# Wider opening matmuls, relu kept in PSUM, more idle matmuls, an output-weight split on VectorE and a changed work order in a fused attention-and-FFN block

## The chip, the cores and the metric

One core of a Trainium2 chip runs the whole kernel. The metric is the device time of one execution in microseconds (us), median of several runs.

## The reference

One encoder layer for 512 tokens of width 1024, in float32. The parts that the kernel's stages follow:

```python
mod = silu(c) @ w_ada + b_ada             # shift, scale, gate for both halves
h = rms_norm(x, norm1_g) * (1 + scale1) + shift1
proj = h @ w_in                           # qa ka va (8 heads of 64), qb kb vb (4 heads of 2x64),
                                          # indexer qi ki wi, gates (2 x 1024)
idx_score = sum_h wi_h * relu(qi_h . ki)  # per query and key; top 256 keys are kept for branch A
y_a = softmax(norm(qa).norm(ka)/8 - alibi, on the kept keys) @ va
y_b = rms_norm((softmax_1 - lam*softmax_2) @ vb)
merged = sigmoid(g_a) * (y_a @ w_up_a) + sigmoid(g_b) * (y_b @ w_up_b)
x = x + gate1 * (merged @ w_o)
h2 = rms_norm(x, norm2_g) * (1 + scale2) + shift2
out = x + gate2 * ((silu(h2 @ w_ff1) * (h2 @ w_ff3)) @ w_ff2)
```

## The kernel before

Every large product is made of three fp32r matmuls: each operand is split into a high half (a cast on ScalarE, `cp`) and a low half (the difference, on VectorE by `sb` or on GpSimd by `psub`), and `Bank.three` adds high x high, high x low and low x high in PSUM. Weights come from HBM in units of 128x1024 (`load`, tiles `raw`), and `split` makes tiles `whi` and `wlo` of them; `ON_DVE` lists the kinds of unit whose low half is made on VectorE, the others go to GpSimd.

The program is written as a list of operations with their inputs, outputs and a cost in ns. `Order.plan` simulates the engines with these costs, takes on each engine the ready operation with the lowest priority number, and so fixes the order of every engine's instructions. `moved(d)` shifts the priority of what is inside. The order on the chip is then fixed: an engine that waits for one instruction runs none of those behind it. PSUM has three pools: `mm` (4 banks), `sb` (2) and `tb` (2).

Stages, by the time of the profile:

1. Opening (0 to 58 us). x is normalised (`scale_x`; `XS` lists the row blocks that ScalarE scales, VectorE takes the others), and for each of 8 column blocks `cb` the conditioning columns are made (`ada_col`: two reductions over 512 KB each on VectorE), x is transposed and scaled (`make_h`), and TensorE adds the block's part of q and k of B heads 0 and 1 (`quad_mm`: 128x256 each, tiles `qb`, `kb`) and of the indexer (`stat_mm`, tile `idx`). Six `idle` matmuls in float32 run before the first real one.
2. Indexer scores and attention (58 to 310 us). `scores` multiplies q and k of the indexer, ScalarE writes the relu into an SBUF tile `relu`, VectorE weights and adds it; `select` finds the top 256 keys in 16 rounds on VectorE. The heads are `head_b` and `head_a`. `quad` makes the other q, k, v projections in matmuls of 256 columns, `quad_out` normalises and transposes them. `PROG` is the list that sets the order in which all this is created; between the heads stand gate projections (`g0` to `g15`).
3. Gates and up-projections (to 382 us), `gate` and `up`, with `ada_late` (`l2`, `l99`): it makes the gate row of the first half (`ada_row`) and then the eight conditioning columns of the second half (`ada_col(1, ...)`).
4. Output projection (382 to 439 us), tiles `wo`; `split_o` splits its weights, the low halves on GpSimd (`psub`).
5. FFN (439 to 795 us), tiles `ff`.

The lines that set the order in stages 2 and 3:

```python
PROG = """scores s8 g0 qb1 vb0 B1 vb1 B0 g3 qa0 g13 g12 kb1 ka0 s9 s8 s9 B2 va0 s99 s8 qa1 g10 B3 g8 ka1 A2 A0 A3 va1
A1 l2 A4 A6 l2 g2 g9 g5 A5 l2 A7 u0 g1 l2 u1 g11 g14 g7 g15 u2 u3 l2 l2 g4 g6 l2 u4 u5 u6 u7 l99"""
```

Of the kernel before, what the change touches and what calls it, by code (L numbers as in the profile page):

```python
# [20 lines left out]
NB = 4  # L21
# [13 lines left out]
QUADS = ["qb0", "kb0", "vb0", "qb1", "kb1", "vb1", "qa0", "ka0", "va0", "qa1", "ka1", "va1"]  # L35
# [3 lines left out]
PROG = """scores s8 g0 qb1 vb0 B1 vb1 B0 g3 qa0 g13 g12 kb1 ka0 s9 s8 s9 B2 va0 s99 s8 qa1 g10 B3 g8 ka1 A2 A0 A3 va1  # L39
A1 l2 A4 A6 l2 g2 g9 g5 A5 l2 A7 u0 g1 l2 u1 g11 g14 g7 g15 u2 u3 l2 l2 g4 g6 l2 u4 u5 u6 u7 l99"""  # L40
# [3 lines left out]
def _units():  # L44
    u = [("p", k) for k in range(8)]
    for w in PROG:
        if w in QUADS:
            u += [(w, 0), (w, 1)]
        elif w[0] == "g":
            u.append(("g", int(w[1:])))  # L50
        elif w[0] == "u":
            u.append(("up", int(w[1:])))
# [25 lines left out]
def _pack(inp):  # L78
# [8 lines left out]
    for i, u in enumerate(UNITS):  # L87
        if u[0] == "p":
            w = w_in[128 * u[1]:128 * u[1] + 128]
            w = np.concatenate([w[:, 3072:3396], w[:, 1536:1792], w[:, 2048:2304]], axis=1)  # L90
        elif u[0] in QUADS:
# [132 lines left out]
class Order:  # L224
# [56 lines left out]
    def plan(self, slots):  # L281
# [19 lines left out]
        while heap:  # L301
# [10 lines left out]
            for e in engs:  # L312
# [65 lines left out]
def _body(ctx: ExitStack, tc: tile.TileContext, a, out):  # L378
# [47 lines left out]
    def act(o, i, n, f=AF.Copy, bias=None, scale=1.0, accum=None, also=()):  # L426
        def fn():
# [4 lines left out]
            else:  # L432
# [3 lines left out]
                if accum is not None:  # L436
# [5 lines left out]
                  after=exps if f == AF.Sigmoid else (), table=table)  # L442
# [51 lines left out]
    def cp(o, i, n):  # L494
        act(o.r(), i, n)
# [156 lines left out]
    def make_h(cb):  # L652
# [3 lines left out]
        for p in range(pieces):  # L656
# [5 lines left out]
            cp(h, f[:, c].k(p), n)  # L662
            sb(l, f[:, c].k(p), h, n)

# [40 lines left out]
    def quad_out(name, banks):  # L705
        kind, br, n = name[0], name[1], int(name[2])
        if kind == "v":
            tl = []
            if br == "a":
                tl = [new("t", "va").rearrange("p (h x) -> p h x", h=4) for _ in range(NB)]  # L710
                src = [banks[t // 2][:, (t % 2) * 256:(t % 2) * 256 + 256].rearrange("p (h x) -> p h x", h=4) for t in range(NB)]
                for q in range(2):
                    for t in (2 * q, 2 * q + 1):
                        cp(tl[t][:, :, 0:64], src[t], 256)
                    for t in (2 * q, 2 * q + 1):
                        sb(tl[t][:, :, 64:128], src[t], tl[t][:, :, 0:64], 256)
            else:
                for q in range(2):
                    h, l = new("t", "vbh"), new("t", "vbl")
                    cp(h, banks[q], 512)  # L720
                    sb(l, banks[q], h, 512)
                    tl.append((h, l))
# [10 lines left out]
        for q in range(2):  # L733
# [3 lines left out]
            qn.append(s)  # L737
        res = []
        for pr in range(2):
            b = Bank("qkT", "tb")  # L740
            for t in range(NB):
                c = (t % 2) * 256 + pr * P
                b.tr(b[:, t * P:(t + 1) * P], qn[t // 2][:, c:c + P], ident)
# [21 lines left out]
    def gate_out(j, b):  # L765
        gates[j] = new("t", "gate")
        act(gates[j], b, 512)

# [20 lines left out]
    for cb in range(8):  # L789
        ada_col(0, cb)  # L790
        if cb == 7:
# [4 lines left out]
            act(csc, vec[:, V_CC:V_CC + 8], 8, AF.Silu)  # L796
# [3 lines left out]
        with G.moved(-H_MOVE if cb else 0):  # L800
            make_h(cb)
        if cb == 0:
            idle = Bank("idle")
            for _ in range(6):
                G.op("PE", 700, lambda: nc.tensor.matmul(g(idle[:, 0:256]), g(cs[:, 0:P]), g(cs[:, 0:256]), start=True, stop=True),
                     (cs,), (idle,))
            bi = [Bank("idx", x) for x in ("sb", "sb", "tb")]
            bq, bk = [Bank("qb0"), Bank("qb0")], [Bank("kb0"), Bank("kb0")]
# [11 lines left out]
    quad_out("qb0", bq)  # L820
    quad_out("kb0", bk)
# [27 lines left out]
    def scores(i):  # L849
        n = P * (i + 1)  # L850
        for h in range(4):
# [6 lines left out]
            r = new("s", "relu")  # L858
# [59 lines left out]
    def head_b(h):  # L918
        n, pr = h // 2, h % 2
        q, k, v = store[f"qb{n}"][pr], store[f"kb{n}"][pr], store[f"vb{n}"]  # L920
# [328 lines left out]
```

## Time and profile before

| what | value |
|---|---|
| runs | 801.61, 799.69 and 801.50 us, median 801.5 |
| profiled execution | 800.93 us, of which the span from first to last instruction is 799.1 us |
| TensorE busy | 781.9 us of the span, 4261 matmuls |
| VectorE, ScalarE, GpSimd busy | 456.2, 350.1 and 200.3 us |
| mean granted TensorE clock | 0.996 of full |

Busy time is a union of instructions. Matmuls overlap in the pipeline and their ends are modelled, so the distance from one matmul's start to the next one's is the better price of a matmul; an idle time that the profile shows for TensorE is a little shorter than the real one. PE is the matmul itself, PEld the weight load that overlaps it, DVE is VectorE, ACT ScalarE, POOL GpSimd.

### The profile page before, as it was taken

To read this page: it belongs to the slowest core of one execution; us is meant where nothing else is said; L and a number is where in the kernel's file an instruction comes from. 1 tells how busy PE (TensorE), PEld (TensorE's weight loads), DVE (VectorE), ACT (ScalarE), POOL (GpSimd) and SP (SyncE) were. 2 spreads that over 40 slices of the span, in tenths; PEclk is the share of its full clock that TensorE was granted. 3 is DMA by queue.
4 is the path that set the end of the run, shared out by engine and by line. 5 is a ranking of instruction groups with operands and counts; after the bars stand their busy time and mean duration, and the time that the engine had idled before them with its cause. 6 is when DMAs were issued, how large, how long until landed. Compare 5 with 4: busy or idle time off the path is not lost.

```text
span 799.1 us, 11091 instructions
## 1 busy us (share of the span) xinstructions
PE 781.9 (98%) x4261; PEld 673.9 (84%) x4261; DVE 456.2 (57%) x898; ACT 350.1 (44%) x649; POOL 200.3 (25%) x129
## 2 busy tenths in 40 slices
PE   7998999999999999999899999999999999999998
PEld 4997988999999888888688988888888888888886
DVE  5969999855468986277776524444433333212243
ACT  5566486357468777532436422332333322211310
POOL 1036554688464223453920000000000000000000
PEclk8999999999999999999999999999999999999999
DMA  9941222221233312457562223344432232232311
GB/s 348 398 136 53 81 69 65 80 80 65 83 107 117 106 55 87 149 185 279 168 237 80 80 106 112 129 154 153 138 105 85 101 106 84 100 106 85 126 40 66
DMA packets 29147, 97.97 MB, mean 123 GB/s; under 512 B 3235, under 2 KB 4771, under 8 KB 29094
## 3 DMA queue, kind: packets, MB, share of 16 engines
q1 hardware_dynamic: 28518, 96.35, 35.2%
q10 hardware_dynamic: 576, 0.92, 0.3%
q8 instruction: 33, 0.54, 0.3%
q14 instruction: 20, 0.16, 0.1%
HBM read 95.16 MB, written 2.10 MB: 122 GB/s over the span
## 4 chain that ended last, share of the span: by engine, by line
PE 85%; DVE 7%; issue 3%; DMA 2%; ACT 2%; POOL 1%; SPq 0%; POOLq 0%; ACTq 0%; DVEq 0%
PE ff L516 44%; PE gate L516 11%; PE up L516 5%; PE wo L516 3%; PE kb L516 3%; PE qa L516 3%; PE ka L516 2%; PE S L516 2%; PE PT L529 2%; PE qb L516 2%; PE idx L516 2%; PE PVa L516 1%; PE va L516 1%; PE vb L516 1%; DMA raw<-in_wun 1%
## 5 line engine op out<-in xcount | busy, mean ns | idle before, releaser
L429 ACT CAST whi<-raw 128x1024 fp32r<-128x1024 f32 x109 | 114.6, 1052 | 292.3 <-PE ff L516 148.2
L501 POOL TENSOR_TENSOR wlo<-raw,whi 128x1024 fp32r<-128x1024 f32 x46 | 114.9, 2499 | 157.9 <-ACT whi L429 133.3
L453 DVE TENSOR_TENSOR wlo<-raw,whi 128x1024 fp32r<-128x1024 f32 x63 | 77.1, 1225 | 117.4 <-ACT whi L429 114.6
L516 PE MATMUL ff<-h2l,whi 128*128 128x512 f32 (+1 forms) x384 | 142.5, 371 | 0.0
L516 PE MATMUL ff<-h2h,wlo 128*128 128x512 f32 (+1 forms) x384 | 142.4, 371 | 0.0
L516 PE MATMUL ff<-h2h,whi 128*128 128x512 f32 (+1 forms) x384 | 142.3, 372 | 0.0
L516 PE MATMUL ff<-whi,f 128*128 128x512 f32 (+1 forms) x310 | 95.1, 385 | 0.0
L516 PEld LDWEIGHTS ff<-h2l,whi 128*128 128x128 f32 x384 | 72.3, 188 | 12.5
L516 PEld LDWEIGHTS ff<-h2h,wlo 128*128 128x128 f32 x384 | 72.2, 188 | 12.5
L516 PEld LDWEIGHTS ff<-h2h,whi 128*128 128x128 f32 x384 | 72.2, 188 | 12.5
L516 PEld LDWEIGHTS ff<-whi,f 128*128 128x128 f32 x310 | 58.0, 188 | 11.6
L516 PE MATMUL ff<-wlo,f 128*128 128x512 f32 (+1 forms) x155 | 59.5, 385 | 0.0
L459 DVE TENSOR_TENSOR silu<-ff,silu 128x512 f32<-128x512 f32 x22 | 15.2, 692 | 69.4 <-PE ff L516 69.4
L516 PE MATMUL gate<-hh,whi 128*128 128x512 f32 x128 | 51.4, 402 | 0.0
L516 PE MATMUL gate<-hh,wlo 128*128 128x512 f32 x128 | 51.1, 401 | 0.0
L516 PE MATMUL gate<-hl,whi 128*128 128x512 f32 x128 | 51.0, 399 | 0.0
L473 DVE CUSTOM_DVE_ANT_0 raw<-raw,cs 128x1024 f32<-128x1024 f32 x32 | 45.7, 1440 | 4.2 <-DMA raw<-in_adat 2.7
L438 ACT ACTIVATE sx<-sx,nm 128x128 f32<-128x128 f32 (+3 forms) x64 | 35.7, 560 | 9.7 <-DVE nm L473 9.4
L482 POOL TENSOR_TENSOR r<-v,mhalf 128x16 f32<-128x16 f32 (+2 forms) x14 | 27.9, 1993 | 43.9 <-DVE v L463 40.3
L516 PEld LDWEIGHTS ff<-wlo,f 128*128 128x128 f32 x155 | 29.1, 188 | 5.9
L467 DVE SCALAR_TENSOR_TENSOR acc<-raw,csc,acc 128x1024 f32<-128x1024 f32 x16 | 20.7, 1294 | 22.0 <-DMA raw<-in_adar 21.9
L516 PE MATMUL wo<-wo,mh 128*128 128x512 f32 x96 | 30.2, 393 | 1.3 <-ACT mh L429 1.3
(229 smaller groups left out, 1708.0 us busy)
## 6 DMA issues: line engine op xcount, KB each, us to landing
raw<-in_wun SPq DMA_DIRECT2D x118, 512.0 KB, 3.3
raw<-in_adat SPq DMA_DIRECT2D x32, 512.0 KB, 7.3
raw<-in_adar SPq DMA_DIRECT2D x16, 512.0 KB, 3.3
x<-in_x SPq DMA_DIRECT2D x4, 512.0 KB, 5.9
praw<-in_wun SPq DMA_DIRECT2D x8, 256.0 KB, 7.4
xr<-in_x SPq DMA_DIRECT2D x4, 512.0 KB, 5.8
praw<-in_wun SPq DMA_DIRECT2D x8, 162.0 KB, 7.4
out_y<-out SPq DMA_DIRECT2D x4, 256.0 KB, 2.0
```

Of the source, the lines that this page charges most:

```text
L429: nc.scalar.copy(g(o), g(i))
L438: nc.scalar.activation(g(o), g(i), f, scale=g(scale), **kw)
L453: dve(n, False, lambda: nc.vector.tensor_sub(g(o), g(i), g(j)), (i, j), (o,), two=(i, j))
L459: dve(n, False, lambda: nc.vector.tensor_mul(g(o), g(i), g(j)), (i, j), (o,), two=(i, j))
L467: dve(n, False, lambda: nc.vector.scalar_tensor_tensor(g(o), g(i), g(s), g(j), op0=op0, op1=op1), (i, s, j), (o,), len(refs(s)), (i, j))
L473: dve(n, False, lambda: nc.vector.tensor_tensor_reduce(g(o), g(i), g(j), scale, init, op0, op1, g(acc)), (i, j), (o, acc), two=(i, j))
L482: G.op("POOL", 300 + 165 * m, lambda: nc.gpsimd.tensor_tensor(g(o), g(i), g(mhalf[:, 0:1].spread([P, m])), op=ALU.pow), refs(i, mhalf), re ...
L501: G.op("POOL", 147 + 2.106 * n, lambda: nc.gpsimd.tensor_sub(g(o.r()), g(i), g(hi)), (i, hi), (o,), port=True)
L516: lambda: nc.tensor.matmul(g(ap), g(lhsT.r()), g(rhs.r()), start=i == 0, stop=i == self.count - 1), refs(lhsT, rhs), (ap,))
L529: G.op("PE", 109, lambda: nc.tensor.transpose(g(ap), g(in_), g(idt)), refs(in_, idt), (ap,))
```

## The change

- The opening's q and k of B heads 0 and 1, two matmuls of 256 columns, become one of 512 (four banks `bqk`, one for each row block); `qk_out` normalises both together, a first reciprocal root for row blocks 0 and 1 and a second for 2 and 3.
- v of all four B heads is one unit `vb`: 512 columns a matmul, four banks, in place of `vb0` and `vb1` of 256 columns. It stands ahead of `qb1`.
- The relu of the indexer is written back into its PSUM bank, and VectorE reads it there.
- Thirteen idle matmuls in place of six, 60 places later in priority, in a `tb` bank. Row block 0 of x is scaled on ScalarE; a small silu waits until a cast of the first block.
- Low halves of the output weights are made on VectorE.
- The conditioning columns of the second half get a list and a word of their own (`k1`), and stand among `u1` to `g4`; head B3 moves ahead of `qa1`.
- The planner takes a result of ScalarE, VectorE or GpSimd as ready for TensorE 300 ns later than before.

```diff
-QUADS = ["qb0", "kb0", "vb0", "qb1", "kb1", "vb1", "qa0", "ka0", "va0", "qa1", "ka1", "va1"]
+QUADS = ["qb1", "kb1", "qa0", "ka0", "va0", "qa1", "ka1", "va1"]
-PROG = """scores s8 g0 qb1 vb0 B1 vb1 B0 g3 ... B2 va0 s99 s8 qa1 g10 B3 g8 ka1 A2 A0 A3 va1
-A1 l2 A4 A6 l2 g2 g9 g5 A5 l2 A7 u0 g1 l2 u1 g11 g14 g7 g15 u2 u3 l2 l2 g4 g6 l2 u4 u5 u6 u7 l99"""
+PROG = """scores s8 g0 vb qb1 B1 B0 g3 ... B2 va0 s99 s8 B3 qa1 g10 g8 ka1 A2 A0 A3 va1
+A1 l2 A4 A6 l2 g2 g9 g5 A5 l2 A7 u0 g1 l2 u1 k1 g11 k1 g14 k1 g7 k1 g15 k1 u2 k1 u3 k1 g4 k1 g6 u4 u5 u6 u7 l99 k99"""
-ON_DVE = ('f1', 'f3', 'f2', 'p')
+ON_DVE = ('f1', 'f3', 'f2', 'p', 'o')
+PE_SLACK = 300.0
-XS = (1, 2)
+XS = (0, 1, 2)
...
                     x = pick.end + self.HOPS.get((e, d.eng), self.HOP)
+                    if d.eng == "PE" and e in ("ACT", "DVE", "POOL"):
+                        x += PE_SLACK
...
+    def qk_out(nq, nk, banks):
+        out = [[[new("t", "qk") for _ in range(m)] for _ in range(2)] for m in (2, 4)]
+        qn = []
+        for q in range(2):
+            ssq = new("sm", "qss")
+            for t in (2 * q, 2 * q + 1):
+                sq = new("s", "sq")
+                squared = act(sq, banks[t], 512, AF.Square, also=sum(out[0] + out[1], []))
+                c = 8 * (t % 2)
+                rsum(ssq[:, c:c + 8].k(t % 2), sq.rearrange("p (a b) -> p a b", b=64), 512)
+            r = rstd(ssq, 64, 16)
+            for t in (2 * q, 2 * q + 1):
+                s = new("t", "qn")
+                c = 8 * (t % 2)
+                mul(s.rearrange("p (a b) -> p a b", b=64), banks[t].rearrange("p (a b) -> p a b", b=64),
+                    r[:, c:c + 8].spread([P, 8, 64], 2), 512)
+                qn.append(s)
+        for i, name in enumerate((nq, nk)):
+            heads_out(name, out[i], lambda t, pr, i=i: qn[t][:, 256 * i + pr * P:256 * i + pr * P + P], squared)
...
+    def values(name):
+        banks = [Bank(name) for _ in range(NB)]
+        for i in range(4):
+            w = take((name, i))
+            for t in range(NB):
+                for k in (2 * i, 2 * i + 1):
+                    ws, n0 = slice((k % 2) * 512, (k % 2) * 512 + 512), t * P
+                    banks[t].three(banks[t], hs_(hh, k, n0, n0 + P), hs_(hl, k, n0, n0 + P), w[0][:, ws], w[1][:, ws], 512)
...
-            act(csc, vec[:, V_CC:V_CC + 8], 8, AF.Silu)
+            act(csc, vec[:, V_CC:V_CC + 8], 8, AF.Silu, after=(cast,))
-            for _ in range(6):
-                G.op("PE", 700, lambda: nc.tensor.matmul(g(idle[:, 0:256]), g(cs[:, 0:P]), g(cs[:, 0:256]), start=True, stop=True),
-            bq, bk = [Bank("qb0"), Bank("qb0")], [Bank("kb0"), Bank("kb0")]
+            bqk = [Bank("qkb0") for _ in range(NB)]
+            idle = Bank("idle", "tb")
+            with G.moved(60):
+                for _ in range(13):
+                    G.op("PE", 500, lambda: nc.tensor.matmul(g(idle[:, 0:256]), g(cs[:, 0:P]), g(cs[:, 0:256]), start=True, stop=True),
-            quad_mm(bq, w, cb, t, 324, 512)
-            quad_mm(bk, w, cb, t, 580, 512)
+            ws, n0 = slice(324, 836), t * P
+            bqk[t].three(bqk[t], hs_(hh, cb, n0, n0 + P), hs_(hl, cb, n0, n0 + P), w[0][:, ws].k(512), w[1][:, ws].k(512), 512)
...
-            r = new("s", "relu")
+            r = b
             act(r[:, :n], b[:, :n], n, AF.Relu)
...
-    late = [("r", 0, k) for k in range(8)] + [("c", 1, cb) for cb in range(8)]
+    late, late2 = [("r", 0, k) for k in range(8)], [("c", 1, cb) for cb in range(8)]
+    def ada_cols(n):
+        for _ in range(n):
+            if late2:
+                with G.moved(L_MOVE):
+                    ada_col(1, late2.pop(0)[2])
...
-            psub(lo, t[:, kk * 512:kk * 512 + 512], hi, 512)
+            (sb if "o" in ON_DVE else psub)(lo, t[:, kk * 512:kk * 512 + 512], hi, 512)
```

## Rows read from the trace of the kernel before

**Rows 1.** The page: busy time of each engine; the chain that ended last, by engine.

```profile
PE 781.9 (98%) x4261; PEld 673.9 (84%) x4261; DVE 456.2 (57%) x898; ACT 350.1 (44%) x649; POOL 200.3 (25%) x129
...
PE 85%; DVE 7%; issue 3%; DMA 2%; ACT 2%; POOL 1%; SPq 0%; POOLq 0%; ACTq 0%; DVEq 0%
```

**Rows 2.** Stretches: length, busy PE, PEld, DVE, ACT, POOL (instructions); clock; DMA share, GB/s.

```profile
40.00:56.00 16.00, 16.00 (x123) 15.31 (x122) 9.64 (x31) 9.91 (x15) 3.85 (x2) 1.00 0.41 136
...
70.00:100.00 30.00, 27.60 (x216) 26.36 (x215) 29.32 (x79) 14.72 (x24) 14.48 (x11) 1.00 0.21 74
...
320.00:340.00 20.00, 20.00 (x90) 16.52 (x89) 3.78 (x4) 10.76 (x16) 8.74 (x5) 1.00 0.41 142
...
378.00:395.00 17.00, 14.20 (x60) 10.51 (x58) 11.90 (x11) 9.39 (x17) 15.84 (x10) 1.00 0.56 185
```

**Rows 3.** Idle matmuls grouped (ns min/median/max, first and last start); then the first real matmuls, timeline.

```profile
L805 PE MATMUL idle<-cs x12: 498/631/792, 6.2 to 11.1; 128*128 128x256 f32 x12
...
15.95 0.58 PE L516 MATMUL qb<-whi,hh 128*128 128x256 f32 x1 [1.32 <-ACT hh L429]
...
18.04 0.41 PE L516 MATMUL qb<-wlo,hh 128*128 128x256 f32 x1
18.25 0.41 PE L516 MATMUL qb<-whi,hl 128*128 128x256 f32 x1
```

**Rows 4.** Two stretches of 1 us in the opening, columns as in rows 2.

```profile
15.00:16.00 1.00, 0.05 (x1) 0.05 (x1) 1.00 (x3) 1.00 (x5) 0.00 (x0) 0.50 1.10 390
...
21.00:22.00 1.00, 1.00 (x8) 1.00 (x7) 1.00 (x3) 1.00 (x3) 0.00 (x0) 0.72 1.00 397
```

**Rows 5.** Opening: timeline of ScalarE, the chain's indexer pieces, the last indexer matmul.

```profile
20.79 0.62 ACT L429 CAST hh<-xT 128x512 fp32r<-128x512 f32 x1
...
36.84 1.73 PE idx L516 x9
41.84 1.73 PE idx L516 x9
...
57.67 0.33 PE L516 MATMUL idx<-hh,wlo 128*128 128x384 f32 x1
```

**Rows 6.** Timeline of TensorE: first and last of 15, then first and last of 21.

```profile
108.16 0.28 PE L516 MATMUL vb<-whi,hh 128*128 128x256 f32 x1
...
109.83 0.28 PE L516 MATMUL vb<-whi,hl 128*128 128x256 f32 x1
...
349.00 0.39 PE L516 MATMUL gate<-hh,whi 128*128 128x512 f32 x1
...
353.53 0.39 PE L516 MATMUL gate<-hh,wlo 128*128 128x512 f32 x1
```

**Rows 7.** Who waited for whom: us in total, times, longest.

```profile
PE qkT L529 <- DVE qk L453: 1.8, 1, 1.8
PE wo L516 <- POOL wlo L501: 1.4, 1, 1.4
...
PE wo L516 <- ACT mh L429: 1.3, 1, 1.3
...
PEld S L516 <- DVE nm L473: 2.3, 6, 0.7
...
PEld PT L529 <- issue: 1.7, 7, 0.5
```

**Rows 8.** Timeline of VectorE and GpSimd; last, VectorE's subtractions of 512 columns.

```profile
58.28 5.77 POOL L482 TENSOR_TENSOR r<-v,mhalf 128x16 f32<-128x16 f32 x2 [0.18 <-DVE v L463]
...
63.65 1.07 DVE L467 SCALAR_TENSOR_TENSOR sc<-relu,wi,sc 128x256 f32<-128x256 f32 x2
...
67.88 2.40 POOL L501 TENSOR_TENSOR wlo<-raw,whi 128x1024 fp32r<-128x1024 f32 x1 [0.31 <-ACT whi L429]
...
68.10 2.46 DVE L467 SCALAR_TENSOR_TENSOR sc<-relu,wi,sc 128x256 f32<-128x256 f32 x1
...
L453 DVE TENSOR_TENSOR f<-raw,f x6: 683/684/686, 753.8 to 761.1; 128x512 fp32r<-128x512 f32 x6
```

More of the change, by code (lines that the diff above doesn't have):

```diff
@@ L48, in _units @@
             u += [(w, 0), (w, 1)]
+        elif w == "vb":
+            u += [(w, i) for i in range(4)]
         elif w[0] == "g":
@@ L424, in refs, with act @@
         return [x for x in xs if isinstance(x, Ref)]
-    def act(o, i, n, f=AF.Copy, bias=None, scale=1.0, accum=None, also=()):
+    def act(o, i, n, f=AF.Copy, bias=None, scale=1.0, accum=None, also=(), after=()):
         def fn():
@@ L441, in act @@
         op = G.op("ACT", (52 if psum else 94) + 0.833 * n + 93 * k, fn, refs(i, bias, scale), refs(o, accum), also=also,
-                  after=exps if f == AF.Sigmoid else (), table=table)
+                  after=exps if f == AF.Sigmoid else after, table=table)
         if f == AF.Exp:
@@ L661, in make_h @@
             h, l = (x[:, cb, c].k((0, p) if cb == 0 else cb) for x in (hh, hl))
-            cp(h, f[:, c].k(p), n)
+            cast = cp(h, f[:, c].k(p), n)
             sb(l, f[:, c].k(p), h, n)
+        return cast
     def stat_mm(bank, w, k, c=None, m=128, n0=0, n1=512, key=None):
@@ L707, in quad_out @@
         if kind == "v":
[L708 to L722, printed above, removed]
+            tl = [new("t", "va").rearrange("p (h x) -> p h x", h=4) for _ in range(NB)]
+            src = [banks[t // 2][:, (t % 2) * 256:(t % 2) * 256 + 256].rearrange("p (h x) -> p h x", h=4) for t in range(NB)]
+            for q in range(2):
+                for t in (2 * q, 2 * q + 1):
+                    cp(tl[t][:, :, 0:64], src[t], 256)
+                for t in (2 * q, 2 * q + 1):
+                    sb(tl[t][:, :, 64:128], src[t], tl[t][:, :, 0:64], 256)
             store[name] = tl
@@ L737, in quad_out, with heads_out @@
             qn.append(s)
+        heads_out(name, out, lambda t, pr: qn[t // 2][:, (t % 2) * 256 + pr * P:(t % 2) * 256 + pr * P + P], squared)
+    def qk_out(nq, nk, banks):
+        out = [[[new("t", "qk") for _ in range(m)] for _ in range(2)] for m in (2, 4)]
+        qn = []
+        for q in range(2):
+            ssq = new("sm", "qss")
+            for t in (2 * q, 2 * q + 1):
+                sq = new("s", "sq")
[3 more added lines that the diff above has]
+            r = rstd(ssq, 64, 16)
+            for t in (2 * q, 2 * q + 1):
+                s = new("t", "qn")
[5 more added lines that the diff above has]
+            heads_out(name, out[i], lambda t, pr, i=i: qn[t][:, 256 * i + pr * P:256 * i + pr * P + P], squared)
+    def heads_out(name, out, part, squared):
+        kind, br, n = name[0], name[1], int(name[2])
         res = []
@@ L767, in gate_out @@
         act(gates[j], b, 512)
+    def values(name):
[6 more added lines that the diff above has]
+                    banks[t].three(banks[t], hs_(hh, k, n0, n0 + P), hs_(hl, k, n0, n0 + P), w[0][:, ws], w[1][:, ws], 512)
+        store[name] = []
+        for b in banks:
+            h, l = new("t", "vbh"), new("t", "vbl")
+            cp(h, b, 512)
+            sb(l, b, h, 512)
+            store[name].append((h, l))
     def quad(name):
@@ L1114, in _body @@
         else:
[L1115 removed]
+            {"s": select, "A": head_a, "B": head_b, "g": gate, "u": up, "l": ada_late, "k": ada_cols}[w[0]](int(w[1:]))
     ahead(UIX[("o", 3, 1)] + 1)
```

27 lines of the change are left out of this document (14 added, 13 removed).

## Prediction, made before the result

> **What bounds the kernel now.** I read the page first: TensorE is busy for 781.9 of 799.1 us, and the chain that ended last lies 85% on it [rows 1]. So the time is TensorE's own work plus the places where it stands; work on another engine counts only where TensorE waits for it. The second view is the table of stretches [rows 2]: VectorE is full from 70 to 100 us (29.32 of 30), when the scores and the top-256 selection run, but TensorE is still 92% busy then, because projections and gates that need nothing from VectorE lie in between. From 320 to 340 us VectorE works 3.78 of 20 us and TensorE is full: gates and up-projections are left over that run after the last head. So a late attention stage has cover, and what counts are single waits and the price of each matmul. From 378 to 395 us TensorE is busy for only 14.20 of 17 us. The third view is the clock and the timeline of the first 22 us [rows 3, 4], the fourth the list of waits [rows 7]. The FFN is not touched by the change, and I count nothing there.
>
> All sums are made against the profiled execution, 800.93 us (span 799.1 us and 1.8 us around it). The median of the runs, 801.5 us, is 0.6 us above it; I subtract from the median. Differences under 0.3% (2.4 us) can't be told from no change here.
>
> **The opening.** The first real matmul starts at 15.95 us; from 15 to 16 us TensorE was busy for 0.05 us and the granted clock was 0.50, and it returns to full inside 21 to 22 us, the mean there being 0.72 [rows 3, 4]. At that lower level (1.2 GHz) matmuls of 256 columns start 0.21 us apart [rows 3]; at full clock 0.119 us: 15 starts from 108.16 to 109.83 us [rows 6]. The engine had little to do between its last idle matmul (start 11.1 us) and 15.95 us, and then the clock fell. The thirteen idle matmuls are 26 instructions. At the old spacing, (11.1 - 6.2)/11 = 0.445 us, they last 11.6 us, from 6.2 to 17.8 us, past 15.95: the real work would start 1.9 us late. The last idle matmul lasted 498 ns against a median of 631 [rows 3], so its price was about to fall; if the 14 new ones cost half the old spacing, they end at 11.1 + 0.4 + 14 x 0.22 = 14.6 us, before the real work, and leave no pause in which the clock falls. I take this.
>
> With the full clock block 0 is done before block 1 is there: ScalarE ends the high half of block 1 at 20.79 + 0.62 = 21.41 us [rows 5], and block 1 then starts at 21.4 us. From there on the step is 5.00 us a block, from 36.84 to 41.84 us [rows 5], and TensorE sets it: from 40 to 56 us it is busy for 16.00 of 16 us and VectorE for 9.64 [rows 2]. A matmul of 512 columns costs (353.53 - 349.00)/20 = 0.2265 us, two of 256 cost 2 x 0.1193 = 0.2386 us [rows 6], so a pair gains 0.012 us. A block has 12 pairs: 0.14 us, and the step becomes 4.86 us. Seven blocks from 21.41 us end at 55.4 us; before, the last indexer matmul starts at 57.67 us and fills 0.18 us more, 57.85 us. That is 2.4 us. Bounds: with the idle matmuls at the old price the loss at the start is 1.9 us and 8 x 0.14 = 1.1 us comes back, so 0.8 us lost; the best is block 1 earlier by as much as moving a row block's scaling from VectorE to ScalarE may give, which I put at no more than the 0.6 us of a cast of 512 columns [rows 5], so 3.0 us. **Taken: -2.4 us.** The delayed silu is read by the gate row alone, which is made in the middle of the attention stage; the scaling lies beside VectorE's reductions of this stretch; should the scaling be on ScalarE's path, it costs back that 0.6 us.
>
> **v of the B heads.** 192 matmuls of 256 columns become 96 of 512: 96 x 0.012 = 1.2 us. It costs and gains nothing else: as many bytes, four units as before for v and q together, four casts and four differences of 512 columns. Its four banks are all of `mm`, so `qb1` and the gates wait until v is done; that is an exchange of order, and scores and transposes use `sb` and `tb`. **Taken: -1.2 us**, bounds 0.9 and 1.2.
>
> The Trainium skill ("TensorE: Matmul & The Clock Gate", section "Back-to-back issue gap") gives the distance of two matmuls at full clock as N/2.4 ns and a fixed 2.5 ns, so a pair would gain only that 2.5 ns. By it, the 192 pairs give about 0.5 us (an estimate from the page) in place of 2.3 us. The trace has 119 ns for 256 columns where the page gives 109, so I stay with the rows.
>
> **Output weights on VectorE, columns earlier.** TensorE waits 1.4 us there for a difference on GpSimd and 1.3 us for a cast on ScalarE [rows 7], in the stretch where GpSimd is busy for 15.84 of 17 us and VectorE for 11.90 [rows 2]. Twelve differences of 512 columns at 0.684 us [rows 8] and two of twice that width put 12 x 0.684 + 2 x 1.37 = 10.9 us on VectorE. The conditioning columns leave this stretch for the one after `u1`, where VectorE has 16 us free in 20 [rows 2]; with them their transfers leave SP's queue and free the `raw` buffers that the output weights need. Next late is the merge of the last up-projection, which has the first banks' other blocks as cover. Bounds: nothing, where the stall only changes its cause, and 2.7 us. **Taken: -2.4 us**, near the upper end, since both engines waited for lose load.
>
> **Relu in PSUM.** VectorE's weighted sums of 256 columns take 0.53 us each (two in 1.07 us), but one that started while GpSimd ran a 2.40 us difference took 2.46 us [rows 8], 1.9 us longer. Behind it on VectorE stands the work for k's transposes, for which TensorE waits 1.8 us [rows 7]. Reading the relu from PSUM leaves one SBUF input, and such an overlap may go. Against it: a score's bank is now held until VectorE has read it, in the stretch where VectorE is full; and q's transposes now need both reciprocal roots, 5.77/2 = 2.9 us each on GpSimd [rows 8], so k's and q's heads come up to 2.9 us later. Gate 0 (24 matmuls, 5.4 us) and half of `vb` cover that. Bounds: 2.9 us lost, 1.8 us gained. **Taken: -1.0 us.**
>
> **Slack for TensorE, and the new order.** What 300 ns can catch are short waits: S for VectorE's minimum, 2.3 us in 6, and the transposes of the probabilities, 1.7 us in 7 [rows 7], some 0.3 us each. Together 4.0 us is the upper bound; a new order may as well put as much in elsewhere, so the lower bound is 2 us lost (half of it). **Taken: -2.5 us**, as the margin is about the size of the mean wait.
>
> Sum: 2.4 + 1.2 + 2.4 + 1.0 + 2.5 = 9.5 us; 801.5 - 9.5 = **792.0 us** (the profiled execution 791.4). By the upper bounds 3.0 + 1.2 + 2.7 + 1.8 + 4.0 = 12.7, 788.8 us; short waits that the profile hides behind modelled ends may add some us to that.
>
> **Rivals.**
> - *The clock falls all the same*, or the idle matmuls delay the start. For it: their price at full clock is not in the trace. Then the opening loses 0.8 us in place of gaining 2.4: 795.2 us. Chance 0.14.
> - *The stall at the output projection changes its cause*: VectorE works in order, and a difference that waits for a weight's transfer holds the merges of `ml` behind it. For it: TensorE's waits there had two causes, GpSimd and ScalarE [rows 7]. Against: the transfers start earlier. 792.0 + 2.4 = 794.4 us. Chance 0.14.
> - *The new order gives nothing*: the waits of attention only move (slack 0, relu 0), 795.5 us; with 2 us lost, 797.5 us. Chance 0.14.
> - *Slower: VectorE falls behind the order written out for it.* Place: 60 to 160 us. With VectorE at 98% of 70 to 100 us [rows 2] there is no room to catch up; if reading the relu in PSUM and holding its banks puts VectorE behind the plan by X us, TensorE stands X us at the first head's instruction and can't take a gate that stands behind it. It decides when X exceeds 9.5 + 2.4 = 12 us, an eighth of the stretch; at X = 15 us the time is 797 + 10 = 807 us less what the slack absorbs, about 805. Against: the relu concerns 12 short instructions, and waits of TensorE in attention are now few. Chance 0.08.
>
> **How the numbers follow.** The forecast holds 0.50, its own range 787.5 to 794. The three milder cases lie between 794 and 798. The range 787 to 798.5 leaves out the slower case, a little of the third and the low end where many hidden waits go, together below 0.2. Faster by over 0.3% (below 799.1): 0.50 + 0.14 + 0.14 + most of 0.14 = 0.87. Within 0.3%: 0.05. Slower: 0.08.
>
> **What would show it.** In the profile after: granted clock 1.00 from 15 to 22 us and the last indexer matmul at 55 to 56 us; 384 fewer matmuls of 256 columns and 192 more of 512, with starts 0.2265 us apart; no wait of `wo` for GpSimd, and TensorE over 95% busy in the 17 us after the up-projections; no weighted sum of the scores above 1 us on VectorE; fewer waits of S and PT. It is wrong if the clock still reads 0.50 after the first real matmul, if TensorE has a wait of some us between 56 and 75 us for `mm` banks, or if the last up-projection is followed by a wait for `ml`.

## The result, and the profile after

The changed kernel took 807.21 us, median of four runs (805.55 to 808.01); the kernel before took 800.6 us beside it. The ratio is 1.0077, with a 95% interval of 1.0057 to 1.0098: **6.6 us slower**, where 9.5 us faster was forecast. The profiled execution took 808.01 us, its span is 806.0 us.

The page first, as in [rows 1]. TensorE's busy time grew by 5.4 us although it has 178 instructions fewer (192 fewer from the joined matmuls, 14 more idle ones).

```profile
PE 787.3 (98%) x4083; PEld 666.2 (83%) x4083; DVE 465.7 (58%) x911; ACT 351.0 (44%) x650; POOL 174.9 (22%) x115
```

Stretches, columns as in [rows 2, 4]:

```profile
15.00:16.00 1.00, 0.94 (x6) 0.47 (x5) 1.00 (x6) 0.83 (x3) 0.00 (x0) 1.00 1.05 400
...
21.00:22.00 1.00, 1.00 (x8) 0.83 (x7) 1.00 (x3) 1.00 (x3) 0.00 (x0) 1.00 0.98 391
...
240.00:250.00 10.00, 8.08 (x40) 7.74 (x41) 6.86 (x22) 5.24 (x17) 2.53 (x5) 0.66 0.29 105
...
242.00:248.00 6.00, 6.00 (x23) 5.71 (x24) 3.58 (x15) 4.23 (x14) 1.04 (x2) 0.50 0.49 175
...
378.00:395.00 17.00, 14.29 (x60) 10.65 (x58) 15.05 (x23) 10.40 (x18) 2.16 (x1) 0.99 0.68 222
```

The opening does what was forecast: clock 1.00 from 15 to 22 us. The new loss stands in two rows: 240 to 250 us at a mean clock of 0.66 (at 0.50 from 242 to 248 us, though TensorE is busy for all of it), and the output weights' stage, where TensorE is as idle as before and VectorE has taken GpSimd's load.

The two profiled executions can be cut at the same pieces of work. These are the last up-projection and the first matmul of the FFN, before and then after:

```profile
381.41 0.39 PE L516 MATMUL up<-ybh,wlo 128*128 128x512 f32 x1
431.95 0.28 PE L516 MATMUL ff<-h2h,whi 128*128 128x256 f32 x1
...
386.63 0.39 PE L524 MATMUL up<-ybh,wlo 128*128 128x512 f32 x1
439.27 0.28 PE L524 MATMUL ff<-h2h,whi 128*128 128x256 f32 x1
```

With the last indexer matmul (57.67 us in [rows 5], now 55.90 us) and the spans (799.1 and 806.0 us) the difference of 6.9 us splits up: the opening gained 1.8 us, the stretch from there to the last up-projection lost 7.0 us (323.74 us before, 330.73 us after), the output projection lost 2.1 us (50.54 and 52.64 us), and the FFN gained 0.4 us.

TensorE's waits, to be held against [rows 7]:

```profile
PE S L524 <- DVE nm L481: 5.4, 4, 3.4
...
PE wo L524 <- ACT mh L437: 2.2, 2, 1.8
...
PE wo L524 <- ACT whi L437: 0.5, 1, 0.5
...
PE wo L524 <- DVE wlo L461: 0.4, 1, 0.4
```

One wait of 3.4 us for `nm`, a minimum over S that VectorE makes, was not there before. The timeline around it, by engine (TensorE, VectorE, GpSimd, SP's queue):

```profile
238.27 0.28 PE L524 MATMUL va<-whi,hh 128*128 128x256 f32 x1
241.92 1.86 PE L524 MATMUL S<-qk 128*128 128x384 f32 x4 [3.37 <-DVE nm L481]
...
243.79 0.41 PE L524 MATMUL va<-whi,hl 128*128 128x256 f32 x1
244.01 0.41 PE L524 MATMUL va<-whi,hh 128*128 128x256 f32 x1
...
232.65 3.17 DVE L475 SCALAR_TENSOR_TENSOR acc<-raw,csc,acc 128x1024 f32<-128x1024 f32 x1 [3.84 <-DMA raw<-in_adar]
239.23 2.30 DVE L475 SCALAR_TENSOR_TENSOR acc<-raw,csc,acc 128x1024 f32<-128x1024 f32 x1 [3.42 <-DMA raw<-in_adar]
241.57 0.29 DVE L481 CUSTOM_DVE_ANT_0 sx<-S,cst 128x128 f32<-128x128 f32 x1
...
232.34 2.39 POOL L509 TENSOR_TENSOR wlo<-raw,whi 128x1024 fp32r<-128x1024 f32 x1 [3.81 <-ACT whi L437]
238.11 2.35 POOL L509 TENSOR_TENSOR wlo<-raw,whi 128x1024 fp32r<-128x1024 f32 x1 [3.37 <-ACT whi L437]
...
228.55 7.62 SPq L513 DMA_DIRECT2D raw<-in_adar  x2
```

Read from TensorE backwards. S at 241.92 us waits for VectorE's minimum of 241.57 us. That work on VectorE stands behind the product at 239.23 us of the gate row (`ada_row`, word `l2`), and that one waited 3.42 us for its transfer. The transfer was issued late: SP's two issues for the row stretch from 228.55 to 236.17 us, because the second needs a `raw` buffer that the product of 232.65 us frees, and this product took 3.17 us beside a GpSimd subtraction that began 0.31 us before it. After the wait matmuls of 256 columns start 0.21 us apart, as at the lower clock level in [rows 3]. The product at 239.23 us, too, ran beside a GpSimd subtraction (238.11 to 240.46 us) and took 2.30 us, so about 1.0 us of the delay is its own length, and the rest is the late transfer. The price is 3.4 us of wait and, from 242 to 248 us, 6 x (1 - 0.50) = 3.0 us of clock: 6.4 of the 7.0 us that this stretch lost.

### The profile page after: what moved, and what is told of

It reads as the page before. It is cut to its first block, busy times and chain, and to the rows that moved or that the text cites. A ratio compares the mean times of both kernels' runs of the same rounds, so it can differ in the third digit from the quotient of the medians.

```text
span 806.0 us, 10718 instructions
## 1 busy us (share of the span) xinstructions
PE 787.3 (98%) x4083; PEld 666.2 (83%) x4083; DVE 465.7 (58%) x911; ACT 351.0 (44%) x650; POOL 174.9 (22%) x115
## 4 chain that ended last, share of the span: by engine, by line
PE 50%; DVE 5%; DMA 5%; issue 2%; ACT 0%; POOL 0%; SPq 0%; DVEq 0%; POOLq 0%; ACTq 0%
PE ff L524 44%; PE wo L524 4%; DMA raw<-in_adat 3%; DVE raw L481 2%; DMA raw<-in_wun 1%; PE up L524 1%; PE gate L524 1%; DMA raw<-in_adar 1%; DVE wo L461 1%; DVE gate L464 0%; DVE wlo L461 0%; PE h2T L537 0%; DVE gate L467 0%; PE PVa L524 0%; DVE acol L475 0%
## 5 line engine op out<-in xcount | busy, mean ns | idle before, releaser
L461 DVE TENSOR_TENSOR wlo<-raw,whi 128x1024 fp32r<-128x1024 f32 x65 | 79.5, 1223 | 115.8 <-ACT whi L437 113.2
L509 POOL TENSOR_TENSOR wlo<-raw,whi 128x1024 fp32r<-128x1024 f32 x44 | 107.8, 2451 | 163.7 <-ACT whi L437 149.1
L481 DVE CUSTOM_DVE_ANT_0 raw<-raw,cs 128x1024 f32<-128x1024 f32 x32 | 48.4, 1522 | 9.4 <-DMA raw<-in_adat 9.4
L475 DVE SCALAR_TENSOR_TENSOR acc<-raw,csc,acc 128x1024 f32<-128x1024 f32 x16 | 25.3, 1582 | 30.1 <-DMA raw<-in_adar 30.1
L524 PE MATMUL S<-qk 128*128 128x128 f32 (+3 forms) x128 | 31.2, 349 | 5.4 <-DVE nm L481 5.4
```

Of the source, the lines that this page charges most:

```text
L461: dve(n, False, lambda: nc.vector.tensor_sub(g(o), g(i), g(j)), (i, j), (o,), two=(i, j))
L475: dve(n, False, lambda: nc.vector.scalar_tensor_tensor(g(o), g(i), g(s), g(j), op0=op0, op1=op1), (i, s, j), (o,), len(refs(s)), (i, j))
L481: dve(n, False, lambda: nc.vector.tensor_tensor_reduce(g(o), g(i), g(j), scale, init, op0, op1, g(acc)), (i, j), (o, acc), two=(i, j))
L509: G.op("POOL", 147 + 2.106 * n, lambda: nc.gpsimd.tensor_sub(g(o.r()), g(i), g(hi)), (i, hi), (o,), port=True)
L524: lambda: nc.tensor.matmul(g(ap), g(lhsT.r()), g(rhs.r()), start=i == 0, stop=i == self.count - 1), refs(lhsT, rhs), (ap,))
```

## The experiments

Theory A: the added time is this chain, one late gate-row transfer that holds VectorE in its written order. Rivals: the slack (order) as such; the output weights on VectorE; the opening's gain lost in the scores. Eighteen kernels; ratios are to the kernel before on the same chip, so ratios are what is compared across rows ("A" builds on the changed kernel, "B" on the kernel before; five `raw` buffers are always paid for with two 128x512 tiles):

| run | what | median us | ratio, interval |
|---|---|---|---|
| a_norow | A, first gate row's transfers left out | 800.60 | 0.9996, 0.9982 to 1.0009 |
| a_port | A, that row's product as a one-operand sum | 801.05 | 1.0006, 0.9996 to 1.0016 |
| a_rowlate | A, that row later | 811.68 | 1.0140, 1.0115 to 1.0165 |
| a_noslack | A, no slack | 804.60 | 1.0040, 1.0023 to 1.0058 |
| a_wopool | A, output weights on GpSimd | 804.41 | 1.0046, 1.0029 to 1.0064 |
| a_raw5nt | A, five `raw` buffers | 798.03 | 0.9963, 0.9945 to 0.9982 |
| r5_wopool | a_raw5nt, output weights on GpSimd | **795.50** | 0.9944, 0.9929 to 0.9959 |
| r5_noslack | a_raw5nt, no slack | 799.59 | 0.9992, 0.9979 to 1.0005 |
| r5_relusb | a_raw5nt, relu in SBUF | 798.58 | 0.9976, 0.9965 to 0.9986 |
| r5_wopool_nocols | r5_wopool, columns behind the last up | 812.19 | 1.0145, 1.0123 to 1.0166 |
| r5_before | B, five `raw` buffers | 803.67 | 1.0043, 1.0030 to 1.0056 |
| b_open | B and the opening | 802.40 | 1.0032, 1.0017 to 1.0048 |
| b_open_ps | b_open, relu in PSUM | **796.43** | 0.9949, 0.9933 to 0.9965 |
| b_open_slack | b_open, slack | 798.15 | 0.9964, 0.9953 to 0.9976 |
| b_open_both | b_open, relu in PSUM and slack | 798.39 | 0.9972, 0.9959 to 0.9984 |
| b_openvb | b_open and `vb` | 808.90 | 1.0104, 1.0087 to 1.0121 |
| b_openvb_ps | b_open_ps and `vb` | 802.56 | 1.0024, 1.0015 to 1.0034 |
| b_open_ps_wodve | b_open_ps, output weights on VectorE | 801.65 | 1.0009, 1.0000 to 1.0018 |

**The late row.** a_norow keeps the order of every engine and leaves the eight transfers out (so its gate row is another one); a_rowlate moves the words `l2` behind `u0`:

```diff
-        dma(w, a["adar"][s][k], 512)
-        stt(acc, w, csc[:, k:k + 1], acc, ALU.mult, ALU.add, 1024)
+        if s == 0:       # a_norow: no transfer, the product reads the resident tile cs
+            G.op("DMA", 512 * 2.55, lambda: None, (), (w,), lat=DMA_LAG)
+            dve(1024, False, lambda: nc.vector.scalar_tensor_tensor(g(acc), g(cs), ...
...
-A1 l2 A4 A6 l2 g2 g9 g5 A5 l2 A7 u0 g1 l2 u1 k1 g11 k1 g14 k1 g7 k1 g15 k1 u2
+A1 A4 A6 g2 g9 g5 A5 A7 u0 g1 l2 u1 k1 g11 l2 k1 g14 k1 l2 g7 k1 g15 l2 k1 u2
```

> Leaves out the eight transfers of the first gate row (its products are taken with the conditioning tile that is already in SBUF instead), every engine's order as in the changed kernel. Theory A (VectorE waits in order for a late transfer of the gate row, the minima of S behind it hold TensorE for 3.4 us, and the clock then falls for 6.8 us): the wait of S at 238 us goes, the clock stays full there, and the time falls by 5 to 7 us, to 800 to 802 us. Theory B (the whole new order is worse, many small waits): less than 2 us, 805 us or more.

> The changed kernel with the words l2 of the gate row moved behind u0, into the gates and up-projections, where VectorE has time. Theory A: no wait of S for over 1 us near 238 us, 800 to 802 us; if the row's transfers then collide with the conditioning columns, a wait at the output projection of 2 to 4 us comes in its place. Theory B: 805 us or more.

```profile
236.00:245.00 9.00, 8.87 (x68) 8.25 (x67) 7.24 (x25) 7.12 (x20) 4.74 (x6) 1.00 0.20 73
```

Without the transfers (the row above is a_norow's) TensorE has no wait from 236 to 245 us, the clock there stays at 1.00, and the 6.6 us are gone. What comes back is the time of the kernel before and no more: the 9.5 us of the forecast are missing even without the late row. The row later takes the wait at 238 us away too, but its broadcast then waits 2.12 and 2.29 us at 352.5 and 357.6 us and the first merged gate 8.66 us at 396.50 us: in this order the row can't simply go later.

**Which way is it late?** a_port leaves the transfers and the order and changes only what VectorE does with the tile (the sum for the gate row is left out); a_raw5nt gives the transfer another buffer:

```diff
-        stt(acc, w, csc[:, k:k + 1], acc, ALU.mult, ALU.add, 1024)
+        if s == 0:                                 # a_port, first gate row
+            dve(1024, False, lambda: nc.vector.tensor_reduce(g(acc[:, k:k + 1]), g(w), axis=AX.X, op=ALU.add),
...
-NRAW, NW, NT = 4, 3, 36
+NRAW, NW, NT = 5, 3, 34                            # a_raw5nt
```

> The changed kernel with the same order on every engine and the same transfers. For gate row 0, VectorE sums each row tile along its columns instead of multiplying it by a scalar and adding it to the sum (the sum of that gate is left out, so the output is another one). A reduction with one operand in SBUF has taken about 1.2 to 1.3 us where no GpSimd work touched it, the product took 1.29 us alone and 3.17 us beside GpSimd's subtraction at 232.65. Theory A1 (the two engines' shared way into SBUF makes the product long, this frees the row buffer late and sends the next transfer late): the product's place takes about 1.3 us, the next transfer starts some 1.9 us earlier, the wait of TensorE for the minima of S near 238 us falls from 3.4 to under 1.5 us, the clock stays at 1.00 in 240:250 and the median lies at 800 to 803. Theory A2 (the transfer would be late anyway, because the row buffer is filled late): the operation is short, but the wait near 238 stays over 2.5 us, the half clock stays and the median is 805 to 808.

> The changed kernel with five row buffers for raw weights instead of four (and two tiles fewer of 128 by 512 to pay for it), so each transfer can be issued one use earlier. Theory A (VectorE, in the written order, waits for a gate row's transfer that was issued late because a buffer came free late, and the minima of S stand behind it): the wait near 238 us goes or falls under 1 us, no half clock in 240:250, median 799 to 803. Rival B (the row is late because the DMA queue or VectorE itself is full there): the wait stays over 2.5 us and the median stays at 805 to 809. With two tiles fewer, waits of up to 1 us elsewhere are possible.

The timeline of a_port, VectorE, GpSimd, SP:

```profile
231.70 1.22 DVE L1086 TENSOR_REDUCE acc<-raw 128x1 f32<-128x1024 f32 x1 [3.71 <-DMA raw<-in_adar]
236.25 1.22 DVE L1086 TENSOR_REDUCE acc<-raw 128x1 f32<-128x1024 f32 x1 [3.33 <-DMA raw<-in_adar]
...
231.52 2.40 POOL L509 TENSOR_TENSOR wlo<-raw,whi 128x1024 fp32r<-128x1024 f32 x1 [3.81 <-ACT whi L437]
...
227.73 5.54 SPq L513 DMA_DIRECT2D raw<-in_adar  x2
```

GpSimd's subtraction again began before VectorE's instruction, but this one needs one operand from SBUF and takes 1.22 us beside it. The second issue ends at 233.27 us, 0.35 us after the tile is free (236.17 us and the same 0.35 us in the changed kernel). The wait near 238 us is gone, as theory A1 says. a_port shortens both products, so it does not separate the late transfer from the second product's own length. With five buffers the two products lie early and alone, and the time is under that of the kernel before:

```profile
229.47 1.28 DVE L475 SCALAR_TENSOR_TENSOR acc<-raw,csc,acc 128x1024 f32<-128x1024 f32 x1
230.99 1.28 DVE L475 SCALAR_TENSOR_TENSOR acc<-raw,csc,acc 128x1024 f32<-128x1024 f32 x1 [0.24 <-DMA raw<-in_adar]
```

Five buffers with two tiles fewer are no gain of their own in the old order: the kernel before gets slower by them (r5_before; the edit is the same line).

> The kernel before with five row buffers for raw weights and two tiles of 128 by 512 fewer, nothing else. If the fifth buffer only mends the changed kernel's accident (a gate row's transfer issued late, with the minima of S behind it on VectorE), the kernel before, which has no such wait, stays within 1.5 us of its time. Rival: the fifth buffer is a gain of its own in any order (transfers come earlier everywhere, above all in the stage of the output weights, where ScalarE waits for raw weights); then 3 us or more under the kernel before, and nothing of the 798 us is the change's own.

**The slack and the rectifier,** each undone, with four buffers or five:

```diff
-PE_SLACK = 300.0
+PE_SLACK = 0.0                  # a_noslack, r5_noslack
...
-            r = b
+            r = new("s", "relu")   # r5_relusb
```

> The changed kernel with a slack of 0 ns for TensorE. Theory A: the order shifts a little, so the wait at 238 us may go or stay, 800 to 807 us. Theory B (the slack makes the order worse): 799 us or less.

> The changed kernel with five row buffers, and the planner's slack for TensorE's operands set to 0, so the order is another one. If the slack gains by itself (the changed kernel without it was 2.6 us faster only because its accident was smaller), 1 to 3 us slower than 798: 799 to 801. If the slack costs as the pair with four buffers suggests, 795 to 797.

> The changed kernel with five row buffers, and the scores' rectifier written to SBUF instead of back to PSUM; VectorE then reads its operand from SBUF, and the bank is free a step earlier. If the rectifier in PSUM is what keeps the scores' stage from waiting (the opening alone brought 2.2 us of waits for the rectified scores and 2.2 us for the normalised q), the stage from 56 to 100 us takes 1 to 4 us longer and the median is 799 to 802. If the order and the slack did that, it stays within 0.7 us of 798.

The wait at 238 us stays without slack (3.48 us), so the slack isn't its cause. With five buffers it gains 0.3%, some 2.3 us; with four its removal gained 3.0 us by the ratios. In both pairs the intervals just touch. A term that changes sign with the order around it is worth what the order makes of it. Of the short waits that it was to catch it caught little: with five buffers the weight loads of S wait 3.2 us in 5 for the minimum with slack and 3.9 us in 7 without. The rectifier in SBUF costs 1.0 us by the ratios, not told from nothing.

**The output weights.** The edit takes 'o' out of `ON_DVE` or puts it in; r5_wopool_nocols drops the words `k1` and gives the columns back to `late`. It does not restore the old place: the three words `l2` that stood between `u3` and `u4` in the kernel before are missing, so all eight columns go to `l99`, behind `u7`.

> The changed kernel with the low halves of the output weights made on GpSimd again. If VectorE's twelve differences hold the merges back there (the wait of 1.8 us for a cast and the lower clock from 395 to 398 us), the stretch from the last up-projection to the first FFN block gets shorter by 1 to 4 us and the time falls to 803 to 806 us; if the split on VectorE was a gain, it gets longer by 1 to 3 us, 808 to 810 us.

> The changed kernel with five row buffers, but the output weights' low halves on GpSimd, as before the change. With five buffers and VectorE it took 798.0 us. If the move to VectorE gains what the prediction says (a wait of 1.4 us on GpSimd's low half gone), this one is 1 to 2.5 us slower: 799 to 800.5. If the move only changes the wait's cause (VectorE's four subtractions in a row hold the merges of the gates), it stays within 0.7 us; if the move costs, 796 to 797.

> The changed kernel with five row buffers and the output weights' low halves on GpSimd, and the columns of the second set not among the up-projections but, as before the change, after the gate rows of the first set. With the columns among up it took 795.5 us and TensorE had no wait over 0.2 us in the stage of the output weights. If the columns earlier are a gain of their own (the prediction put part of 2.4 us there), 1 to 2.5 us slower: 796.5 to 798, with a wait in 375:400. If the other changes gave that stage its freedom, within 0.7 us.

> The kernel before with the opening's part, the rectifier in PSUM, and the output weights' low halves on VectorE, nothing else. If the prediction's term holds (waits of TensorE for GpSimd's low half and ScalarE's cast gone), 794 to 795. If it costs as in the two pairs measured with the columns among up (2.8 and 2.5 us), 798 to 800, with waits for the merges of the gates in 380:400.

With four buffers the move back gains 2.5 us by the ratios, but some 1.7 us of it are the smaller clock loss from 240 to 250 us (0.83 in place of 0.66); the stage itself gets 1.0 us shorter, although a wait of 2.55 us for GpSimd's low half is back. With five the medians differ by 2.5 us, the ratios by 1.5, and the intervals overlap. The stage shows it: from the end of the last up-projection to the first FFN matmul 51.0 us with VectorE (378.54 to 429.57 us) and 46.7 us with GpSimd (379.78 to 426.49 us), with 217 matmuls in both. So 4.3 us are gained there, and 1.2 us were lost ahead of it, where the last up-projection ends that much later. TensorE from 385 to 395 us, VectorE then GpSimd (the kernels a_raw5nt and r5_wopool):

```profile
385.00:395.00 10.00, 9.14 (x33) 7.06 (x33) 3.93 (x7) 1.34 (x3) 0.00 (x0) 0.83 0.37 135
```

```profile
385.00:395.00 10.00, 9.98 (x44) 7.76 (x44) 5.22 (x8) 1.45 (x4) 6.28 (x5) 1.00 0.75 266
```

The clean pair is b_open_ps_wodve against b_open_ps: 4.8 us slower by the ratios, and one place holds it (TensorE, then VectorE):

```profile
382.46 0.77 PE L524 MATMUL wo<-whi,mh 128*128 128x512 f32 x1 [4.50 <-DVE gate L467]
...
378.02 2.49 DVE L461 TENSOR_TENSOR wo<-raw,wo 128x512 fp32r<-128x512 f32 x4
380.43 0.68 DVE L461 TENSOR_TENSOR ml<-gate,mh 128x512 fp32r<-128x512 f32 x1
381.03 0.68 DVE L461 TENSOR_TENSOR wo<-raw,wo 128x512 fp32r<-128x512 f32 x1
381.63 1.28 DVE L467 TENSOR_TENSOR gate<-up,gate 128x512 f32<-128x512 f32 x2
```

Low halves that are needed later stand ahead of the gate's products in VectorE's order. The columns are the other side of it: put back, their reductions stand on VectorE from 367 to 404 us ahead of the last merges:

```profile
406.24 2.93 PE L524 MATMUL wo<-wo,mh 128*128 128x512 f32 x6 [12.14 <-ACT mh L437]
```

In this order all columns behind the last up-projection cost that wait. In the kernel before, 12 of the 16 reductions had been done by 376 us, so this is no price of the part by itself, and what the columns among up are worth against their old place was not measured.

**The opening by itself, and what carries it.** b_open takes from the diff only the opening (512 columns, idle matmuls, `XS`, `qk_out`); the next three add the rectifier, the slack, or both, two more the word `vb`:

```diff
-            r = new("s", "relu")
+            r = b                   # b_open_ps, b_open_both, b_openvb_ps
...
-PE_SLACK = 0.0
+PE_SLACK = 300.0                # b_open_slack, b_open_both
...
-scores s8 g0 qb1 vb0 B1 vb1 B0 g3 ...
+scores s8 g0 vb qb1 B1 B0 g3 ...    # b_openvb, b_openvb_ps
```

> The kernel before with the opening's part of the change alone: 13 idle matmuls of half the count of columns each, q and k of the first heads as matmuls of 512 columns, their new normalisation. All else as before. By the profile of the changed kernel the opening won about 1.8 us of clock and 0.1 us of step: median 1.5 to 3 us under the kernel before. If the opening's gain is lost in the scores that follow (the extra normalisation on VectorE at 60 to 100 us), within 0.5 us of it.

> The kernel before with the opening's part alone (802.4 us, 1.5 us over the kernel before; TensorE waited 2.2 us for a normalised q and 2.2 us for a rectified score, each with 3.4 us of half clock behind it), and the rectifier written back to PSUM. If the rectifier's detour through SBUF makes those waits, they go and the median falls to 797 to 799.5. If the order of VectorE makes them (the planner sees the new normalisation too early), the waits stay and the median is 801 to 804.

> The kernel before with the opening's part alone and the planner's slack of 300 for TensorE's operands, the rectifier in SBUF as before. If the waits of 2.2 us at 61.9 and in 80:90 come from an order without slack, both go and the median falls to 797 to 800; if they come from the rectifier, they stay and it is 801 to 804.

> The kernel before with the opening's part, the rectifier in PSUM and the slack, without the values as 512 columns, the output weights on VectorE and the columns among up. If the prediction's terms add up (opening 2.4, rectifier 1.0, slack 2.5) it is 5 us or more under the kernel before: 794 to 796. If the slack and the rectifier only take back what the opening brought on the scores, 798 to 800. If a new order brings its own accident as it did twice (a wait over 2 us and a half clock behind it), over 801.

> The kernel before with the opening's part and the values of the B heads as matmuls of 512 columns; the order of the other work, the weights' low halves, the rectifier and the planner's costs as before. If the matmuls' start distances decide (0.227 us for 512 columns against twice 0.120 for 256), 1.2 us under the opening alone, so 3 to 4 us under the kernel before. If four banks of PSUM held at once delay what stands beside them, no gain or a loss of up to 2 us against the opening alone.

> The kernel before with the opening's part, the rectifier in PSUM (these two alone took 796.43 us) and the values of the B heads as matmuls of 512 columns, without slack, with the output weights and the columns where they were. If the values' term holds (1.2 us less work for TensorE) and the order brings nothing, 795.2 us. If holding four banks at once, or S of the first heads earlier against VectorE, costs what the profile of the changed kernel shows at 106 to 109 us (1.7 us of waits for the minima of S), 796.5 to 798. If the order of the later heads stays as bad as with the rectifier in SBUF (808.9), over 801.

The opening alone is slower. Its timeline, TensorE, VectorE, GpSimd; the last line is the operation of the third VectorE line as the kernel before shows it:

```profile
64.49 0.36 PE L537 MATMUL qkT<-vec,qn 128*128 128x128 f32 x1 [2.22 <-DVE qn L467]
...
80.68 0.73 PE L524 MATMUL score<-ki,qi 128*128 128x512 f32 x2 [2.20 <-ACT relu L446]
...
60.16 3.55 DVE L475 SCALAR_TENSOR_TENSOR sc<-relu,wi,sc 128x256 f32<-128x256 f32 x2
63.74 1.29 DVE L467 TENSOR_TENSOR qn<-qkb,r 128x512 f32<-128x512 f32 x2
78.15 1.78 DVE L471 TENSOR_SCALAR sc<-relu,wi 128x384 f32<-128x384 f32 x1
...
61.07 2.36 POOL L509 TENSOR_TENSOR wlo<-raw,whi 128x1024 fp32r<-128x1024 f32 x1
77.35 2.37 POOL L509 TENSOR_TENSOR wlo<-raw,whi 128x1024 fp32r<-128x1024 f32 x1 [1.67 <-DVE m L920]
...
77.98 0.41 DVE L463 TENSOR_SCALAR sc<-relu,wi 128x384 f32<-128x384 f32 x1
```

Two weighted sums that read the relu in SBUF take 3.55 us beside GpSimd's subtraction, and the normalised q comes late. The second wait has a like cause: the first weighting of the next block took 1.78 us beside another subtraction, against 0.41 us alone. With the relu in PSUM (b_open_ps) two such sums take 1.06 us beside longer GpSimd work, and the whole is 6.6 us faster by the ratios:

```profile
61.83 1.28 DVE L467 TENSOR_TENSOR qn<-qkb,r 128x512 f32<-128x512 f32 x2
63.03 1.06 DVE L475 SCALAR_TENSOR_TENSOR sc<-score,wi,sc 128x256 f32<-128x256 f32 x2
...
62.06 4.75 POOL L509 TENSOR_TENSOR wlo<-raw,whi 128x1024 fp32r<-128x1024 f32 x2
```

The slack alone also takes both waits of 2.2 us away (0.9964; the longest from 54 to 110 us is 0.88 us); both together are no better than either. `vb` costs 6.0 us on top of b_open_ps and 5.8 us on top of b_open by the ratios, where 1.2 us of gain were expected. In b_openvb_ps S of the first heads waits 0.53 and 1.19 us for VectorE:

```profile
108.20 0.50 PE L524 MATMUL S<-qk 128*128 128x256 f32 x2 [1.19 <-DVE nm L481]
```

The mean clock is 0.94 from 100 to 130 us, and the later B heads lose another 2.3 us from 213 to 219 us (0.17, 0.29 and 0.31 us for VectorE and 1.54 us for GpSimd). The rest of this cost was not traced to single waits. The same pair of waits stands in the changed kernel (0.51 and 1.21 us at 107.3 and 109.0 us) and in b_openvb (0.75 and 0.98 us), while the four kernels with the opening and without `vb` have at most one wait of S from 98 to 125 us, of 0.7 us or less: the pair comes with `vb` and its place in the order.

## Why the prediction was wrong

**The step that failed** is "Slack for TensorE, and the new order", -2.5 us with 2 us lost as the worst. The worst of a new order was sized by half of its hoped gain; nothing in the rows bounds it that way. Measured, one accident of the new order cost 5.7 to 6.5 us (a_port, a_norow, by the ratios), and the slack itself stands between 2.3 us gained and 3.0 us lost.

That step explains why the change made the kernel slower, and not the whole miss. Forecast and result are 16.1 us apart; without the accident the kernel is level with the one before, and about 9.5 us are still missing. Second in size is the output projection: 2.4 us shorter was forecast, 2.1 us longer was measured. The best that was reached, the changed kernel with five buffers and the output weights back on GpSimd, gained 4.5 us by the ratio, where the forecast without the output weights' term is 7.1 us.

**The rival "VectorE falls behind the order written out for it"** named the right mechanism, VectorE in order with TensorE standing behind it, and missed its place (232 to 241 us, not 60 to 160), its cause (a late transfer and two collisions with GpSimd, not a full VectorE) and the point from which it decides. It asked for 12 us of delay, because it let the 9.5 us of gain stand. They were not there, and so a wait of 3.4 us, with 3.0 us of clock behind it that the rival had not counted, was enough.

**Output weights on VectorE: -2.4 us** was wrong in sign. The wait for GpSimd went, as said; VectorE's order put low halves ahead of the gates' merges, which is the rival "changes its cause", at a loss rather than at nothing: 4.8 us in the clean pair, 1.5 us in the pair with five buffers, 1.0 us of the stage with four. TensorE is busy for 14.29 of 17 us there, not 95%.

**The opening: -2.4 us** was right in its mechanism up to its own end. The clock stays full. The idle matmuls end later than the 14.6 us of the sum (the last one starts at 15.4 us) and the first real matmul starts at 16.53 us, 0.6 us later than before, at full clock. The last indexer matmul starts here:

```profile
55.90 0.34 PE L524 MATMUL idx<-hh,wlo 128*128 128x384 f32 x1
```

That is 1.8 us earlier than [rows 5]. The step was mis-sized: 4.96 us a block (39.64 to 44.60 us), not 4.86. In the opening the joined matmuls start (39.41 - 37.09)/10 = 0.232 us apart, in `vb` (76.19 - 73.69)/11 = 0.227 us:

```profile
37.09 0.39 PE L524 MATMUL qkb<-wlo,hh 128*128 128x512 f32 x1
...
39.41 0.40 PE L524 MATMUL qkb<-whi,hl 128*128 128x512 f32 x1
39.64 0.39 PE L524 MATMUL idx<-hh,whi 128*68 128x512 f32 x1
...
44.60 0.39 PE L524 MATMUL idx<-hh,whi 128*68 128x512 f32 x1
...
73.69 0.39 PE L524 MATMUL vb<-whi,hl 128*128 128x512 f32 x1
...
76.19 0.39 PE L524 MATMUL vb<-wlo,hh 128*128 128x512 f32 x1
```

So by these distances the 192 pairs give 96 x 0.011 + 96 x 0.007 = 1.7 us, where the rows of before gave 2.3 us. The Trainium skill ("TensorE: Matmul & The Clock Gate", section "Back-to-back issue gap"), from which the prediction estimated 0.5 us, calls its formula that of an isolated matmul. The opening shows less than its part of the 1.7 us: from the indexer matmul marked `128*68` in the third block to the same one in the seventh it took 19.99 us before (31.64 to 51.63 us) and 19.86 us after (29.70 to 49.56 us), so 0.03 us a block were gained and not 0.14. The lead was 1.9 us at the third block already and 1.8 us at the end, so the gain is the start at the full clock. What the step left out is that an earlier end is worth something only if VectorE's next work is ready for it: alone, the opening made the time 0.3% longer.

**Values: -1.2 us** was right as work (1.1 us by the distances) and wrong as "costs and gains nothing else": the whole part lost 5.8 and 6.0 us where it was measured, and in the changed kernel the two waits of S that come with it are 1.7 us.

**Relu in PSUM: -1.0 us** had the right mechanism (no weighted sum of the changed kernel is above 0.74 us). Its size depends on whether a collision is there to be removed: 1.0 us on a_raw5nt (not told from nothing), 6.6 us on b_open, beyond the bound of 1.8.

The terms do not add: 0.9949 and 0.9964 together gave 0.9972. What remains open is whether the width of `vb` or its place in the order makes the waits of S at 107 to 109 us, and how far each measured part would keep its value in another order.

## What to carry to other kernels

In a kernel whose engines run a fixed order, a reordering can cost more than it was hoped to gain: single waits of 3.4 to 12.1 us came up here, behind a late transfer or behind work that was written down too early. So look for products whose operand comes late from memory and which stand ahead of short work on TensorE's path. Price a wait with the clock that followed it in the trace. Give the part that removes a collision (an operand in PSUM, one more buffer) before the parts that reorder: the opening and the relu in PSUM alone took 796.43 us, and the changed kernel with five buffers and the output weights on GpSimd 795.50 us, both faster than either kernel.

## What the runs showed of the hardware

A VectorE instruction with two operands in SBUF that started 0.31 us after a GpSimd subtraction took 3.17 us instead of 1.28; a reduction with a single SBUF operand took 1.22 us in the same place, and two weighted sums with one operand in PSUM took 1.06 us together. The Trainium skill ("SBUF — State Buffer", section "Who interferes with whom") says that an instruction of VectorE with two SBUF inputs contends with one of GpSimd that reads SBUF, and that one with at most one such input does not, unless it runs in one of VectorE's two-port modes. These runs agree on both kinds above. One SBUF operand alone is no safeguard here either: a `TENSOR_SCALAR` with one such tile took 1.78 us beside a subtraction and 0.41 us alone. Whether it ran in a two-port mode no trace here shows.

Unexpected was what such 2 us become: a late buffer, a transfer issued 0.35 us after it came free, a wait of 3.4 us on TensorE, and then the clock at its lower level (0.50 of full, 1.2 GHz) from 242 to 248 us, though TensorE was busy again from 241.92 us.
